# Moving the block inverses, the key and query steps and the first norm of a two-layer hybrid encoder

## The chip, the cores and the metric

The kernel runs on one core of a Trainium2 chip, as one program. The metric is the device time of one execution in microseconds (us); the time given for a kernel is the median over its runs. Besides the runs that are timed there is one profiled execution, whose trace gives start, duration and waits of every instruction. TensorE is written PE, its weight loads PEld, VectorE DVE, ScalarE ACT, GpSimd POOL and SyncE SP.

## The reference

The input is 1024 tokens of width 1024, with 16 learned tokens in front: 1040 columns. Each of two layers adds a mixer and a SwiGLU feed-forward part to the residual. The mixer has four heads of a delta rule that runs forward and backward over the sequence, and a short gated convolution beside them.

```python
h = concat([meta, x])                                   # 1040 x 1024
for l in range(2):
    y = rmsnorm(h, norm1_w[l])
    qkv, z, b, a, sc_b, sc_c, sc_h = split(y @ w_in[l])
    q, k, v = split(silu(depthwise_conv3(qkv, conv_qkv_w[l])))
    q, k = l2norm(q), l2norm(k)                         # per head of 128
    beta, g = sigmoid(b), -exp(a_log) * softplus(a + dt_bias)
    o = delta(q, k, v, g[fwd], beta[fwd]) + flip(delta(flip(q, k, v), g[bwd], beta[bwd]))
    o = o * rsqrt(mean(o * o) + eps) * dn_norm_w * silu(z)   # per head
    y_sc = sc_b * depthwise_conv3(sc_c * sc_h)
    h = h + concat([o, y_sc]) @ w_out[l]
    h = h + swiglu(rmsnorm(h, norm2_w[l]))
return rmsnorm(h, final_norm_w)[16:]

def delta(q, k, v, g, beta):       # in chunks of c rows
    G = cumsum(g);  D = exp(G_i - G_j), i >= j
    A = 1 + strictly_lower((beta k) k^T * D)
    u, w = A^-1 (beta v), A^-1 (beta k exp(G))
    attn = (q k^T * D) / sqrt(128);  qd = q exp(G) / sqrt(128)
    for each chunk:
        v_new = u - w S
        o = qd S + attn v_new
        S = S * exp(G_last) + (k exp(G_last - G))^T v_new
```

Since `q` enters `o` linearly, a factor on a query row is a factor on the output row, and the norm of the output divides it out but for `eps`.

## The kernel before

The tokens lie along the free dimension: 1040 columns, in three column chunks of 348, 346 and 346 (`FULL`; the second layer's last products use `TAIL`, without the first 16). Every large product is computed in fp32r with both operands split into a high and a low part: `dense` issues three matmuls per block of 128 input rows, 24 for one output tile of 128 and one column chunk (L154 to L156 for high by high, high by low, low by high). `wsplit` makes the weight parts, the high part on ScalarE (L127), the low part on GpSimd or, where `lov[0]` is set, on VectorE (L128).

A planner decides the order: each engine has a queue that runs in order, and the order in it is set when the kernel is built, from a priority that each instruction has when it is issued and from the planner's own idea of when its inputs are there. The code sets these priorities by hand. From the value tiles on, dense products get a low priority and serve as filling (`mmp[0]`, `low`), and evictions of them have their own (`evp[0]`). After each dense chunk `dense` pops one function from the list `jobs`, and so small work gets a place between two dense chunks.

A layer goes through these steps.

1. The norm. In the first layer the columns are scaled and split as they arrive. `add_sq` squares the eight tiles and adds them up on VectorE, GpSimd and ScalarE (L173 and near), `finish_rstd` sums over partitions with three products by a matrix of ones (L192), and the first two projections are multiplied by the result afterwards. The other norms use `finish_bc`: four column groups of a matrix of ones, then a row to memory and a broadcast back (L205).
2. The input projection, tile by tile in the order key (4 to 7), query (0 to 3), value (8 to 11), then gates `z` and the short convolution. Each tile is evicted, convolved, and passed through SiLU. `sums` (L590) adds up the squares of a key or query head; after the fourth head `normalise` takes the root, sends the row through memory to all partitions (`bc`, in a ring of two 128x1040 buffers named "c") and multiplies the four heads (L404).
3. `chunk_p` (L431), for each of nine chunks of the sequence (one of 16 columns and eight of 128): key products, decay matrix (loaded from memory, added to, four exponentials), and the product of the two for both directions. Three chunks are issued in a row.
4. `sub_start` and `substitute(d)` (L518, L520): 31 steps of two VectorE operations invert the diagonal blocks of 32 in all 32 matrices of direction d at once. For the backward direction the two 128x1024 operands (`x`) lie in the ring "c".
5. `invert(d)`: from blocks of 32 to 64 to 128. Each stage is a row of small products (L549, L555, L561 of 32x32; L573, L575 of 64x64), and evictions on ScalarE (L551, L557, L563, L577, L579) that feed the next stage. `invert(0)` is issued behind value tile 0, `substitute(1)` behind tile 1 and `invert(1)` behind tile 2, all its stages with a priority of their own ahead of the dense products.
6. `chunk_a`, for each of nine chunks: the query-key products (L474), `eg` (a broadcast load that ScalarE issues, L478) times the queries (L479), and `dt` (loaded too) times the products (L484); the results go to memory. Three chunks are issued behind each of value tiles 1 to 3.
7. The scan: `scan_step(d, c)` has chains of products with evictions between them (L762 and near). An order written by hand, below, puts three forward steps first, then mixes the directions, and ends with backward steps alone. The second layer's backward scan is one step shorter. When both directions of a chunk are there, `finalize` adds them, normalises by root mean square (four squares, root, reciprocal), turns the result and multiplies by the gate.
8. The output projection. The half that comes from the convolution channels fills TensorE during the scan; the other half (`out_part`) follows when the scan is over.
9. The second norm and the feed-forward part, as products of sums in the manner of Strassen. The change does not touch it.

```python
order = [(0, s) for s in range(3)]
for i in range(6):
    order += [(1, i), (0, 3 + i)]
order += [(1, s) for s in range(6, nb)]
```

Of the kernel before, what the change touches and what calls it, by code (L numbers as in the profile page):

```python
# [15 lines left out]
KT = 8  # L16
NMETA = 16
L = 1040
# [22 lines left out]
def trunk(ctx: ExitStack, tc: tile.TileContext, xT, w_in, w_ba, w_out, w_gu, w_dn,  # L41
# [76 lines left out]
    jobs = []  # L118
# [24 lines left out]
    def dense(ws, xs, chunks, evac, pool=None):  # L143

        for (n0, n1) in chunks:
            n = n1 - n0
            ps = (pool or pacc)()
            K = len(xs)
            here = tc.cur_priority
            if mmp[0] is not None:  # L150
                at_prio(mmp[0])
            for k in range(K):
                (wh, wl), (xh, xl) = ws[k], xs[k]
                mm(ps[:, :n], wh, xh[:, n0:n1], start=(k == 0), stop=False)  # L154
                mm(ps[:, :n], wh, xl[:, n0:n1], start=False, stop=False)  # L155
                mm(ps[:, :n], wl, xh[:, n0:n1], start=False, stop=(k == K - 1))  # L156
# [39 lines left out]
    def finish_bc(ss, n0, n1, dst):  # L196

        e = (n1 - n0) // 4
        ps = bank("a")
        for j in range(4):  # L200
            mm(ps[32 * j:32 * j + 32, 0:e], ones[:, 0:32], ss[:, n0 + e * j:n0 + e * j + e], start=True, stop=True, skip_group_check=True)
        r = c4k("r")[:, 0:e]
        act(out=r, in_=ps[:, 0:e], func=AF.Sqrt, scale=1.0 / D, bias=cols["eps"])
        nc.vector.reciprocal(out=r, in_=r)
        dma(dst[:, 0:e], r.rearrange("(a b) c -> a b c", b=32)[:, 0, :])  # L205
# [30 lines left out]
    for m in range(KT):  # L236
        add_sq(hv[m], ss, m == 0, (ptt, tt)[m % 2], m % 2 == 1, lasts[6])
# [15 lines left out]
    epsq = sb.tile([128, 1], F32, name="epsq")  # L253
    nc.vector.memset(epsq, HD * EPS)
# [5 lines left out]
    finish_rstd(ss, FULL)  # L260

    hsrc = xT
    for l in range(DEPTH):
# [129 lines left out]
        def normalise(dst, l2, r):  # L393

            scale, bias = ((float(HD), epsq), (1.0, epsc))[r > 0]
            r4 = row(Y[1] + "f")[:, 0:260]
            act(out=r4, in_=l2[:, 0:260], func=AF.Sqrt, scale=scale, bias=bias)
# [124 lines left out]
        def invert(d):  # L522
# [17 lines left out]
            def fb():  # L540
                return bank("fb"[d]).rearrange("p (q c) -> p q c", c=32)

            for qh in range(2):
                qs = slice(16 * qh, 16 * qh + 16)
                qr = range(16 * qh, 16 * qh + 16)
                ps = fb()
                for q in qr:
                    for (f, s) in pairs:
                        mm(ps[B[s], q - 16 * qh, :], P_[B[f], q, B[s]], XB[B[f], q, :], start=True, stop=True, skip_group_check=True)  # L549
                for (f, s) in pairs:  # L550
                    act(out=QS[B[s], qs, :], in_=ps[B[s]], func=AF.Copy, scale=-1.0)  # L551
                ps = fb()
                for q in qr:
                    for (f, s) in pairs:
                        mm(ps[B[f], q - 16 * qh, :], QS[B[s], q, :], P_[B[s], q, B[s]], start=True, stop=True, skip_group_check=True)  # L555
                for (f, s) in pairs:
                    act(out=P_[B[f], qs, B[s]], in_=ps[B[f]], func=AF.Copy)  # L557
                f, s = pairs[0]
                ps = fb()
                for q in qr:  # L560
                    mm(ps[B[s], q - 16 * qh, :], P_[B[s], q, B[s]], QS[B[s], q, :], start=True, stop=True)  # L561
                fo, so = 32 * (f % 2), 32 * (s % 2)
                act(out=X64[B[s], qs, fo:fo + 32], in_=ps[B[s]], func=AF.Copy)  # L563
                nc.vector.tensor_copy(X64[B[f], qs, fo:fo + 32], XB[B[f], qs, :])
                nc.vector.tensor_copy(X64[B[s], qs, so:so + 32], XB[B[s], qs, :])
                nc.vector.memset(X64[B[f], qs, so:so + 32], 0.0)

            F_, S_ = (slice(0, 64), slice(64, 128)) if d == 0 else (slice(64, 128), slice(0, 64))
            for qh in range(5):
                p1, p2 = [(bank("fb"[d]).rearrange("p (q c) -> p q c", c=64) if on else None) for on in (qh < 4, qh > 0)]  # L570
                for q in range(8):
                    if qh < 4:
                        mm(p1[S_, q, :], P_[F_, 8 * qh + q, S_], X64[F_, 8 * qh + q, :], start=True, stop=True)  # L573
                    if qh > 0:
                        mm(p2[F_, q, :], X64[S_, 8 * qh - 8 + q, :], P_[S_, 8 * qh - 8 + q, S_], start=True, stop=True)  # L575
                if qh < 4:
                    act(out=X64[S_, 8 * qh:8 * qh + 8, :], in_=p1[S_], func=AF.Copy, scale=-1.0)  # L577
                if qh > 0:
                    act(out=P_[F_, 8 * qh - 8:8 * qh, S_], in_=p2[F_], func=AF.Copy)  # L579
            at_prio(sub_end)  # L580


        l2s = {}

        def sums(which, q, sq_):
# [5 lines left out]
            if q == 3:  # L591
                normalise(*((KTt, l2s["k"], 4) if which == "k" else (QT, l2s["q"], 0)))

        seq = (4, 5, 6, 7, 0, 1, 2, 3)
        for pos, i in enumerate(seq):
# [12 lines left out]
            act(out=dst, in_=dst, func=AF.Silu)  # L608
            act(out=t, in_=dst, func=AF.Square)
            jobs.append(lambda w="qk"[i >= 4], q=hh, t=t: sums(w, q, t))  # L610
# [54 lines left out]
        for i in range(4):  # L665
            t = trow()
            inproj(8 + i, to_row(t))
# [45 lines left out]
        evp[0] = None  # L713

# [89 lines left out]
        def finalize(c, n, s0, po, pof):  # L804
# [15 lines left out]
            act(out=st[0:n], in_=st[0:n], func=AF.Sqrt, scale=1.0 / HD, bias=epsc[0:n])  # L820
# [486 lines left out]
```

## Time and profile before

| | before |
|---|---|
| median of 3 runs | 2667.32 us (2663.91 to 2669.51) |
| profiled execution | 2669.32 us, its span 2667.5 us |
| TensorE busy, weight loads | 2559.5 us (96%), 2343.7 us (88%) |
| VectorE, ScalarE, GpSimd busy | 1528.0 (57%), 988.5 (37%), 1088.5 us (41%) |
| mean granted TensorE clock | 0.981 |
| mean DMA traffic | 122 GB/s |

The page shows the span in forty slices of 66.7 us, a digit for the busy share of each in tenths; the row PEclk is the granted clock of TensorE in the same manner. Layer 0 runs from 0 to about 1380 us, layer 1 behind it. A group of the page is one line of the kernel on one engine: count, busy time, mean duration in ns, and the idle time of the engine just before its instructions, with what ended it. In a timeline the same is given for single instructions or short rows of them. Matmuls overlap, so their durations add up to more than the time that passes: of two dense products behind each other the starts are to be compared. One fp32 product of TensorE shows as two records.

### The profile page before, as it was taken

To read this page: it belongs to the slowest core of one execution; us is meant where nothing else is said; L and a number is where in the kernel's file an instruction comes from. 1 tells how busy PE (TensorE), PEld (TensorE's weight loads), DVE (VectorE), ACT (ScalarE), POOL (GpSimd) and SP (SyncE) were. 2 spreads that over 40 slices of the span, in tenths; PEclk is the share of its full clock that TensorE was granted. 3 is DMA by queue.
4 is the path that set the end of the run, shared out by engine and by line. 5 is a ranking of instruction groups with operands and counts; after the bars stand their busy time and mean duration, and the time that the engine had idled before them with its cause. 6 is when DMAs were issued, how large, how long until landed. Compare 5 with 4: busy or idle time off the path is not lost. (4 is left out here: it accounts for less than half of the span.)

```text
span 2667.5 us, 43943 instructions
## 1 busy us (share of the span) xinstructions
PE 2559.5 (96%) x17274; PEld 2343.7 (88%) x17274; DVE 1528.0 (57%) x2265; ACT 988.5 (37%) x1785; POOL 1088.5 (41%) x803
## 2 busy tenths in 40 slices
PE   8889899999999999999999998999989999999997
PEld 7889899999999999999999887898877888887886
DVE  6688333648765566522356873336497766654226
ACT  4664222425333333321246642235353333332224
POOL 3142121225766666533221321212367666663341
PEclk9999799999999999999999998999999999999999
DMA  3442685434312222532224425856232222225321
GB/s 107 143 138 83 206 252 185 144 122 138 108 60 79 85 72 76 193 111 69 73 93 142 154 76 176 280 181 207 95 126 93 68 80 77 89 88 184 93 81 64
DMA packets 181636, 326.27 MB, mean 122 GB/s; under 512 B 21696, under 2 KB 58948, under 8 KB 181428
## 3 DMA queue, kind: packets, MB, share of 16 engines
q1 hardware_dynamic: 148116, 272.77, 31.1%
q10 hardware_dynamic: 30496, 42.09, 5.2%
q0 software_dynamic: 2816, 8.59, 1.0%
q8 instruction: 136, 2.23, 0.4%
q14 instruction: 72, 0.59, 0.1%
HBM read 239.79 MB, written 83.58 MB: 121 GB/s over the span
## 5 line engine op out<-in xcount | busy, mean ns | idle before, releaser
L128 POOL TENSOR_TENSOR wlo<-raw,whi 128x512 fp32r<-128x512 f32 x244 | 294.6, 1210 | 941.2 <-ACT whi L127 857.5
L154 PE MATMUL pacc<-a,whi 128*128 128x346 f32 (+2 forms) x1031 | 347.3, 340 | 10.6 <-ACT whi L127 7.5
L127 ACT ACTIVATE whi<-raw 128x512 fp32r<-128x512 f32 (+2 forms) x264 | 151.5, 577 | 540.5 <-PE pacc L155 302.1
L156 PE MATMUL pacc<-a,wlo 128*128 128x346 f32 (+2 forms) x1031 | 347.8, 340 | 1.5 <-DVE wlo L128 0.9
L155 PE MATMUL pacc<-a,whi 128*128 128x346 f32 (+2 forms) x916 | 311.8, 341 | 1.2 <-DVE a L853 1.1
L154 PE MATMUL pacc<-b,whi 128*128 128x346 f32 (+2 forms) x882 | 303.3, 345 | 1.7 <-ACT whi L127 1.1
L156 PE MATMUL pacc<-b,wlo 128*128 128x346 f32 (+2 forms) x882 | 301.0, 344 | 0.0
L155 PE MATMUL pacc<-b,whi 128*128 128x346 f32 (+2 forms) x776 | 265.8, 343 | 1.1 <-DVE b L853 1.1
L154 PEld LDWEIGHTS pacc<-a,whi 128*128 128x128 f32 x1031 | 197.4, 192 | 22.6 <-ACT whi L127 8.7
L156 PEld LDWEIGHTS pacc<-a,wlo 128*128 128x128 f32 x1031 | 197.9, 192 | 9.9 <-DVE wlo L128 1.6
L155 PEld LDWEIGHTS pacc<-a,whi 128*128 128x128 f32 x916 | 176.1, 192 | 9.4 <-DVE a L853 1.7
L154 PEld LDWEIGHTS pacc<-b,whi 128*128 128x128 f32 x882 | 166.3, 189 | 14.9 <-issue 2.5
L156 PEld LDWEIGHTS pacc<-b,wlo 128*128 128x128 f32 x882 | 165.9, 188 | 10.4 <-issue 0.8
L996 POOL TENSOR_TENSOR wlo<-rw,whi 128x512 fp32r<-128x512 f32 x92 | 135.8, 1479 | 73.3 <-ACT whi L995 66.1
L155 PEld LDWEIGHTS pacc<-b,whi 128*128 128x128 f32 x776 | 146.6, 189 | 10.5 <-DVE b L853 1.3
L996 POOL TENSOR_TENSOR a<-rw,a 128x512 fp32r<-128x512 f32 x64 | 105.7, 1654 | 64.4 <-ACT a L995 61.7
L996 POOL TENSOR_TENSOR b<-rw,b 128x512 fp32r<-128x512 f32 x64 | 90.2, 1412 | 85.2 <-ACT b L995 54.5
L858 DVE TENSOR_TENSOR a<-pacc,a 128x346 f32<-128x346 f32 (+2 forms) x116 | 57.7, 500 | 113.6 <-PE pacc L156 112.4
L858 DVE TENSOR_TENSOR b<-pacc,b 128x512 f32<-128x512 f32 (+1 forms) x88 | 52.5, 600 | 108.4 <-PE pacc L156 107.8
L995 ACT ACTIVATE whi<-rw 128x512 fp32r<-128x512 f32 x92 | 57.8, 631 | 140.9 <-DVE rw L1069 69.9
L1070 DVE TENSOR_TENSOR rw<-raw,rw 128x512 f32<-128x512 f32 x44 | 98.0, 2227 | 1.2
L996 POOL TENSOR_TENSOR wlo<-raw,whi 128x512 fp32r<-128x512 f32 x50 | 77.5, 1552 | 34.5 <-ACT whi L995 25.9
(814 smaller groups left out, 7348.1 us busy)
## 6 DMA issues: line engine op xcount, KB each, us to landing
raw<-in_w_in SPq DMA_DIRECT2D x112, 256.0 KB, 3.0
raw<-in_w_gu SPq DMA_DIRECT2D x104, 256.0 KB, 2.7
rw<-in_w_gu SPq DMA_DIRECT2D x88, 256.0 KB, 2.6
rec<-aqd SPq DMA_DIRECT2D x62, 256.0 KB, 4.5
rec<-vkd SPq DMA_DIRECT2D x61, 256.0 KB, 2.9
raw<-in_w_dn SPq DMA_DIRECT2D x60, 256.0 KB, 2.6
raw<-in_w_out SPq DMA_DIRECT2D x48, 256.0 KB, 2.9
a<-ad SPq DMA_DIRECT2D x20, 520.0 KB, 4.6
```

What stands on the lines that cost most here:

```text
L127: act(out=hi, in_=raw[:, 0:kk, :], func=AF.Copy)
L128: (tt if lov[0] else ptt)(out=lo, in0=raw[:, 0:kk, :], in1=hi.bitcast(F32), op=ALU.subtract)
L154: mm(ps[:, :n], wh, xh[:, n0:n1], start=(k == 0), stop=False)
L155: mm(ps[:, :n], wh, xl[:, n0:n1], start=False, stop=False)
L156: mm(ps[:, :n], wl, xh[:, n0:n1], start=False, stop=(k == K - 1))
L858: tt(out=hr[m][:, n0:n1], in0=ps, in1=hr[m][:, n0:n1], op=ALU.add)
L995: act(out=hi, in_=src, func=AF.Copy)
L996: ptt(out=lo, in0=src, in1=hi.bitcast(F32), op=ALU.subtract)
L1070: tt(out=A21, in0=A11, in1=A21, op=ALU.subtract)
```

## The change

- **Inverses in pieces.** `invert(d)` no longer issues its stages. It returns seven functions: the three 32-blocked stages, each for both halves of the matrices, and the 64-blocked stages in four parts of two quarters each. They stand in the new list `jobs3`, and one is popped behind each dense chunk: those of `invert(0)` from value tile 3 on, those of `invert(1)` from the fourth of the tiles behind the values on. Their products are issued through `low`, with the priority of the dense products. `substitute(1)` is issued behind the first of these tiles.
- **Key and attention products by chunk.** `chunk_p` and `chunk_a` stand in `jobs2`, one chunk of the sequence behind each dense chunk: `chunk_p` from the fourth key tile on, `chunk_a` from value tile 2 on.
- **Queries unnormed.** The queries are not divided by their length. The sums of squares of the four heads are issued together, behind the last query tile; `query_lengths` sends the sums through memory into 36 rows of 128, turns them on TensorE, scales them and keeps them in `g`, which is free by then. `finalize` adds the length to the mean square of the output in place of `eps`.
- **First squares on TensorE.** ScalarE squares each of the eight tiles, and 32 products of 260 columns sum over partitions and tiles in one bank, in two jobs behind the second and third dense chunk; `finish_bc` goes on from there.
- **Scan order.** Four forward steps come first, and so four backward steps last (three in the second layer, before two).
- `lov[0]`, with which VectorE makes the low weight parts, stays set for the value tiles and two tiles behind them.

```diff
-            if jobs:
-                jobs.pop(0)()
+            for q in (jobs, jobs2, jobs3):
+                f = q.pop(0) if q else None
+                if f is not None:
+                    f()
...
-    def finish_bc(ss, n0, n1, dst):
+    def finish_bc(ss, n0, n1, dst, ps=None):
...
-        ps = bank("a")
-        for j in range(4):
+        sums = ps is None
+        ps = bank("a") if sums else ps
+        for j in range(4 if sums else 0):
...
-    for m in range(KT):
-        add_sq(hv[m], ss, m == 0, (ptt, tt)[m % 2], m % 2 == 1, lasts[6])
+    def first_sums(m0):
+        if m0 == 0:
+            fps.append(bank("b"))
+        for m in range(m0, m0 + 4):
+            sq = c4k("sq")
+            act(out=sq, in_=hv[m], func=AF.Square)
+            for j in range(4):
+                mm(fps[0][32 * j:32 * j + 32, 0:260], ones[:, 0:32], sq[:, 260 * j:260 * j + 260], start=(m == 0), stop=(m == KT - 1), skip_group_check=True)
+        if m0 == 4:
+            finish_bc(ss, 0, L, dram.tile([4, 260], F32, name=nm("rsd")), fps[0])
+
+    jobs.extend([None, lambda: first_sums(0), lambda: first_sums(4)])
...
-    finish_rstd(ss, FULL)
...
-            sub_end = tc.cur_priority
-            at_prio(base - 20000 + 1000 * d)
...
+            def first():
+                for qs in halves:
+                    ps = fb(32)
+                    low(lambda: [mm(ps[B[s], q - qs.start, :], P_[B[f], q, B[s]], XB[B[f], q, :], start=True, stop=True, skip_group_check=True)
+                                 for q in range(qs.start, qs.stop) for (f, s) in pairs])
                     for (f, s) in pairs:
+                        act(out=QS[B[s], qs, :], in_=ps[B[s]], func=AF.Copy, scale=-1.0)
...
+            def fourth(qh):
+                ps = fb(64)
+                low(lambda: [mm(ps[S_, q, :], P_[F_, 8 * qh + q, S_], X64[F_, 8 * qh + q, :], start=True, stop=True) for q in range(8)])
+                act(out=X64[S_, 8 * qh:8 * qh + 8, :], in_=ps[S_], func=AF.Copy, scale=-1.0)
...
+            return [first, second, third] + [lambda f=f, q=q: [f(q), f(q + 1)] for q in (0, 2) for f in (fourth, fifth)]
...
-            if q == 3:
-                normalise(*((KTt, l2s["k"], 4) if which == "k" else (QT, l2s["q"], 0)))
+            if q == 3 and which == "k":
+                normalise(KTt, l2s["k"], 4)
+            elif q == 3:
+                query_lengths(l2s["q"])
+
+        def query_lengths(l2):
+            r4 = t2k("r4").rearrange("p a b -> p (a b)")[:, 0:260]
+            nc.vector.tensor_copy(r4, l2[:, 0:260])
+            for h in range(H):
+                qdma(rnd[h].rearrange("(a c) -> a c", a=4), r4.rearrange("(a b) c -> a b c", b=32)[:, h, :])
+            rows = t2k("rows").rearrange("p a b -> p (a b)")[0:36, 0:128]
+            for h in range(H):
+                qdma(rows[9 * h:9 * h + 1, 0:16], rnd[h:h + 1, 0:16])
+                qdma(rows[9 * h + 1:9 * h + 9, :], rnd[h, 16:L].rearrange("(c p) -> c p", p=128))
+            def turn():
+                ps = pa()
+                low(lambda: nc.tensor.transpose(ps[:, 0:36], rows, ident[0:36, 0:36]))
+                ts(out=g[:, 0].rearrange("p c h -> p h c"), in0=ps[:, 0:36].rearrange("p (h c) -> p h c", h=4), scalar1=HD * EPS, scalar2=HD * EPS * EPS, op0=ALU.mult, op1=ALU.add)
+            jobs.append(turn)
...
-            if pos == 4:
+            if pos == 3:
+                jobs.append(None)
                 jobs.extend([lambda c=c: k_out(c) for c in range(9)])
-            if pos in (4, 5, 6):
-                for c in range(3 * pos - 12, 3 * pos - 9):
-                    chunk_p(c)
+                jobs2.extend([None, None] + [lambda c=c: chunk_p(c) for c in range(9)])
+
+        for hh in range(4):
+            lengths("q", hh, QT[:, hh, :], c4k("sq"))
+        qs_ = jobs[-4:]
+        del jobs[-4:]
+        jobs.extend([None, None, None, lambda: [f() for f in qs_]])
         sub_start()
         substitute(0)
...
+            if i == 2:
+                jobs2.extend([lambda c=c: chunk_a(c) for c in ca])
+            if i == 3:
+                jobs3.extend(invert(0))
             inproj(8 + i, to_row(t))
...
-            if i == 0:
-                invert(0)
-            elif i == 1:
-                substitute(1)
-                lov[0] = False
-            elif i == 2:
-                invert(1)
-            if i > 0:
-                for c in ca[3 * i - 3:3 * i]:
-                    chunk_a(c)
...
         for j, q in enumerate((4, 5, 0, 6, 7, 1, 2, 3)):
+            lov[0] = j < 2
+            if j == 3:
+                jobs3.extend(invert(1))
...
+            if j == 0:
+                substitute(1)
...
-            act(out=st[0:n], in_=st[0:n], func=AF.Sqrt, scale=1.0 / HD, bias=epsc[0:n])
+            stt(out=st[0:n], in0=st[0:n], scalar=1.0 / HD, in1=g[0:n, 0, c, :], op0=ALU.mult, op1=ALU.add)
+            act(out=st[0:n], in_=st[0:n], func=AF.Sqrt)
...
-        order = [(0, s) for s in range(3)]
-        for i in range(6):
-            order += [(1, i), (0, 3 + i)]
-        order += [(1, s) for s in range(6, nb)]
+        order = [(0, s) for s in range(4)]
+        for i in range(5):
+            order += [(1, i), (0, 4 + i)]
+        order += [(1, s) for s in range(5, nb)]
```

More of the change, by code (lines that the diff above doesn't have):

```diff
@@ L538, in invert @@
             X64 = tmp[:, 0:2, :].rearrange("p a b -> p (a b)")[:, 0:2048].rearrange("p (q c) -> p q c", q=32)
[L540 to L547, printed above, removed]
-                    for (f, s) in pairs:
[L549 to L553, printed above, removed]
+            halves = [slice(0, 16), slice(16, 32)]
@@ L554, in invert, with second @@
+            def second():
+                for qs in halves:
+                    ps = fb(32)
+                    low(lambda: [mm(ps[B[f], q - qs.start, :], QS[B[s], q, :], P_[B[s], q, B[s]], start=True, stop=True, skip_group_check=True)
+                                 for q in range(qs.start, qs.stop) for (f, s) in pairs])
                     for (f, s) in pairs:
-                        mm(ps[B[f], q - 16 * qh, :], QS[B[s], q, :], P_[B[s], q, B[s]], start=True, stop=True, skip_group_check=True)
@@ L556, in invert, with third @@
-                for (f, s) in pairs:
-                    act(out=P_[B[f], qs, B[s]], in_=ps[B[f]], func=AF.Copy)
+                        act(out=P_[B[f], qs, B[s]], in_=ps[B[f]], func=AF.Copy)
+            def third():
                 f, s = pairs[0]
-                ps = fb()
-                for q in qr:
-                    mm(ps[B[s], q - 16 * qh, :], P_[B[s], q, B[s]], QS[B[s], q, :], start=True, stop=True)
                 fo, so = 32 * (f % 2), 32 * (s % 2)
-                act(out=X64[B[s], qs, fo:fo + 32], in_=ps[B[s]], func=AF.Copy)
@@ L580, in invert @@
-            at_prio(sub_end)
+                for qs in halves:
+                    ps = fb(32)
+                    low(lambda: [mm(ps[B[s], q - qs.start, :], P_[B[s], q, B[s]], QS[B[s], q, :], start=True, stop=True) for q in range(qs.start, qs.stop)])
+                    act(out=X64[B[s], qs, fo:fo + 32], in_=ps[B[s]], func=AF.Copy)
+                    nc.vector.tensor_copy(X64[B[f], qs, fo:fo + 32], XB[B[f], qs, :])
+                    nc.vector.tensor_copy(X64[B[s], qs, so:so + 32], XB[B[s], qs, :])
+                    nc.vector.memset(X64[B[f], qs, so:so + 32], 0.0)
@@ L607, in trunk @@
             conv(t, dst, P_CV + 3 * i)
[L608 to L610 removed]
+            if i >= 4:
+                lengths("k", hh, dst, t)
             if pos == 2:
```

33 lines of the change are left out of this document (14 added, 19 removed).

## The prediction

> **What bounds the kernel now.** I read the page first, then the tables by stretch, the engine timelines of the stretches that stood out, the groups by line, and one tile. The page:
>
> ```profile
> span 2667.5 us, 43943 instructions
> PE 2559.5 (96%) x17274; PEld 2343.7 (88%) x17274; DVE 1528.0 (57%) x2265; ACT 988.5 (37%) x1785; POOL 1088.5 (41%) x803
> PEclk9999799999999999999999998999999999999999
> ```
>
> TensorE is the bound: 96% of the span, so what can be won lies in its 108 us of idle time and in the slices where the clock row falls to 7 and 8. The profiled execution took 2669.32 us, 1.8 us around its span; the median of the runs is 2667.32, 2.0 below it, so the sum below is made against 2669.32 and carried over by subtracting 2.0. The table by stretch (length, then busy time of TensorE, its weight loads, VectorE, ScalarE, GpSimd, clock, DMA share, GB/s) shows where they lie:
>
> ```profile
> 0.00:62.00 62.00, 50.47 (x274) 44.13 (x275) 44.70 (x44) 30.12 (x36) 21.20 (x14) 1.00 0.34 115
> ...
> 164.00:284.00 120.00, 113.73 (x1057) 106.88 (x1055) 98.85 (x184) 51.79 (x68) 31.05 (x26) 0.99 0.30 95
> 284.00:352.00 68.00, 57.97 (x658) 55.23 (x659) 24.25 (x36) 19.68 (x30) 8.61 (x6) 0.75 0.73 239
> 352.00:560.00 208.00, 205.90 (x1482) 199.84 (x1482) 98.49 (x231) 76.76 (x221) 47.94 (x30) 0.99 0.57 187
> ...
> 1614.00:1656.00 42.00, 32.64 (x487) 27.79 (x486) 13.32 (x17) 14.12 (x22) 4.92 (x3) 0.72 0.54 174
> ```
>
> The rows 284:352 (layer 0) and 1614:1656 (layer 1) hold the backward inverse, `invert(1)`, and stand out: 10.0 and 9.4 us idle and a granted clock of 0.75 and 0.72. The scan behind it (352:560) idles 2.1 us in 208 and needs nothing. The same table for the time at half clock:
>
> ```profile
> 293.80:321.10 27.30, 22.96 (x294) 21.38 (x293) 10.21 (x12) 13.25 (x20) 3.67 (x2) 0.50 0.59 197
> 345.00:351.80 6.80, 6.09 (x23) 6.02 (x24) 2.46 (x4) 0.00 (x0) 0.00 (x0) 0.50 1.03 332
> 1628.40:1652.30 23.90, 18.00 (x249) 16.21 (x250) 9.17 (x10) 11.34 (x17) 2.36 (x1) 0.50 0.42 138
> 300.60:307.40 6.80, 6.80 (x131) 6.74 (x130) 2.58 (x4) 3.52 (x5) 0.00 (x0) 0.50 0.65 217
> ```
>
> TensorE's timeline shows why (start, duration, what, [idle before <- who ended it]):
>
> ```profile
> 284.45 1.20 PE L549 MATMUL pb<-b,P 32*32 32x32 f32 x64 [1.65 <-DVE dt L484]
> ...
> 293.25 0.66 PE L660 MATMUL pa<-ident,b3f 128*128 128x128 f32 x4 [1.16 <-ACT b3f L661]
> 297.23 1.92 PE L549 MATMUL pb<-b,P 32*32 32x32 f32 x64 [2.73 <-ACT P L557]
> ...
> 345.70 1.65 PE L474 MATMUL pb<-b,b 128*128 128x128 f32 x6 [3.56 <-DVE dt L484]
> ...
> 1629.54 1.92 PE L549 MATMUL pb<-a,P 32*32 32x32 f32 x64 [3.19 <-ACT P L557]
> ...
> 1638.73 3.67 PE L573 MATMUL pb<-a,P 64*64 64x64 f32 x32 [1.47 <-ACT P L557]
> ```
>
> Each stage of the inverse waits for the eviction of the stage before it, with no dense product between, and its small products do not hold the clock: one stage that takes 1.20 us at 284 takes 1.92 at 297.
>
> **Inverses in seven pieces.** In the changed kernel's instruction order, TensorE has 24 dense products (one chunk of 346 columns) between any two pieces of `invert(1)`, in both layers; before, all its later stages stood in a row. What goes: layer 0, idle 10.0, and half of the busy time at half clock, (22.96 + 6.09) / 2 = 14.5, together 24.5; layer 1, 9.4 + 18.00 / 2 = 18.4. Sum 42.9 us. The work itself stays.
>
> What comes back is bounded by zero and by the same 19.4 us of waits again. I take the rate of the row 164:284, where the forward inverse already runs between dense products: 6.27 idle in 120, 5.2%, over the 110 - 43 = 67 us that the two stretches then last, 3.5 us. The clock: a piece of the first two kinds is now 64 small products without a break, two groups like the 1.20 us one at 284.45, 2.4 us. Four inverses have eight such pieces. If none trips the clock it costs 0, if each costs one step of 3.4 us at half speed (the two rows of 6.8 us are two steps each) 8 x 1.7 = 13.6. At 284.45 a single group did not trip it at once, so I take two of eight: 3.4 us.
>
> Here the Trainium skill ("TensorE: Matmul & The Clock Gate", section "What's actually happening") says that the clock halves after an idle window of about 3.4 us and comes back after a busy one. By that rule no piece could trip it, and the sum would be 3.4 us lower. The row 300.60:307.40 disagrees: busy for 6.80 of 6.80 us, in small products, at 0.50.
>
> **Key products, attention products and queries.** `chunk_p` goes from bunches of three to one behind each dense chunk at nearly the same place: nothing on the path. The larger effect comes with the queries. Before, `chunk_a` needed normalised queries, and these needed the broadcast buffers that `substitute(1)` holds; so it ran after it, on top of the inverse. Now it needs only the raw queries, and in the new order most of its multiplies stand among the 62 + 62 substitution steps on VectorE. VectorE's groups from 160 to 352 us (count | busy, mean ns | idle before, releasers):
>
> ```profile
> L520 DVE TENSOR_TENSOR b<-b,Tm 128x31 f32<-128x31 f32 (+15 forms) x31 | 15.6, 502 | 0.7
> L520 DVE TENSOR_TENSOR x<-x,Tm 128x31 f32<-128x31 f32 (+15 forms) x31 | 14.8, 476 | 0.9
> ...
> L518 DVE TENSOR_TENSOR Tm<-b 128x31 f32<-128x31 f32 (+15 forms) x31 | 12.5, 404 | 0.7
> L518 DVE TENSOR_TENSOR Tm<-x,x 128x31 f32<-128x31 f32 (+15 forms) x31 | 11.5, 371 | 0.9
> L479 DVE TENSOR_TENSOR eg<-b,eg 128x512 f32<-128x512 f32 x13 | 9.3, 719 | 19.3 <-DMA eg<-ged 14.6 <-DMA aqd<-eg 2.6 <-issue 2.0
> L484 DVE TENSOR_TENSOR dt<-pb,dt 128x512 f32<-128x512 f32 x13 | 8.8, 688 | 19.3 <-PE pb L474 10.0 <-DMA dt<-dtd 5.9 <-issue 2.8
> L404 DVE TENSOR_TENSOR b<-b,bc 128x1040 f32<-128x1040 f32 x4 | 5.4, 1360 | 4.0 <-DMA bc<-rnd 4.0
> ...
> L128 DVE TENSOR_TENSOR wlo<-raw,whi 128x512 fp32r<-128x512 f32 x1 | 0.7, 692 | 0.2 <-ACT whi L127 0.2
> ```
>
> Is VectorE then the bound? In 164:284 it is busy 98.85 us. Added: 32 large multiplies of `chunk_a` at 0.70, 22.4 (some 3 us of them were in the stretch), eight weight splits moved over from GpSimd at 0.69, 5.5; removed, the four query multiplies, 5.4. That makes about 119 us. TensorE's own time for the stretch up to the backward inverse grows from 120 to about 134: the order has 49 more dense products there (7.8 us at 0.16 each) and some 24 chunk products and 24 transposes (about 6). VectorE stays some 15 us ahead, so I cost the move at nothing; the cover is those 15 us. The two new query transposes are 0.3 us (four transposes take 0.66 at 293.25). The length in the output norm is one 128x4 operation in each of 17 steps, behind the scan's dense products. GpSimd's queue gets twelve small transfers for four 128x1040 ones; the turn that needs them stands some 200 products later, so nothing waits.
>
> **First squares on TensorE.** The rows of the old way, and what a group of four 260-column sums costs:
>
> ```profile
> 28.07 0.43 PE L155 MATMUL pacc<-a3f,whi 128*128 128x348 f32 x1 [2.28 <-DVE a3f L173]
> ...
> 40.45 0.85 PE L192 MATMUL pa<-rstd,ones 128*128 128x348 f32 x2 [0.20 <-DVE rstd L184]
> 41.14 1.33 PE L192 MATMUL pb<-rstd,ones 128*128 128x346 f32 x4
> ```
>
> ```profile
> 1394.26 0.33 PE L154 MATMUL pacc<-b,whi 128*128 128x346 f32 x1
> 1394.42 0.32 PE L155 MATMUL pacc<-b,whi 128*128 128x346 f32 x1
> 1394.67 0.65 PE L590 MATMUL pf<-a,sel 128*32 128x260 f32 x8
> 1395.24 0.43 PE L156 MATMUL pacc<-b,wlo 128*128 128x346 f32 x1
> 1395.51 0.32 PE L154 MATMUL pacc<-b,whi 128*128 128x346 f32 x1
> ```
>
> From L155 at 1394.42 to the second dense product behind it, at 1395.51, it is 1.09 us; without the sums it would be two steps of 0.16 (1394.26 to 1394.42). A group adds 0.77, eight 6.2; the three old sums, 2.0, go, and the 2.28 wait goes because VectorE no longer squares between the splits. Of the 11.5 us idle in 0:62, the sums can fill some. Against it, the norm now goes through memory. As at the next layer's norm,
>
> ```profile
> 1368.88 0.52 SPq L205 DMA_DIRECT2D rsd<-r  x1
> ```
>
> ```profile
> 1374.38 1.26 DVE L605 TENSOR_TENSOR a<-a,rstd 128x1040 f32<-128x1040 f32 x1 [1.21 <-DMA rstd<-rsd]
> ```
>
> 5.5 us pass before its first use, and on ScalarE's queue a weight cast for the third tile stands behind the first convolution that needs it: I reckon TensorE waits about 2.5 us. All of it on the path gives +6.7 (6.2 - 2.0 + 2.5), all of it in idle time -5; I take -1.
>
> **Sum.** 2669.3 - 42.9 + 3.5 + 3.4 + 0.3 - 1 = 2632.6, and 2.0 less for the median: 2630.6 us, a gain of 36.7. Its own range, 2620 to 2648: below, no waits and no half clock (-6.9) and the start at its best (-4); above, half of the waits and of the trips return, (19.4 + 13.6) / 2 - 6.9 = 9.6, and the start at its worst, 7.7.
>
> **Rivals.**
> A, slower: the multiplies of `chunk_a` take their waits along. The two groups above wait 38.6 us in layer 0 for their loads and products; VectorE's queue runs in order, so the substitution behind them waits too, and then every piece of the inverse. It decides from 15 us of such waits in a layer, and the kernel is slower from 15 + 36.7 / 2 = 33. At the full 38.6 it is 2 x (38.6 - 15) = 47 us: 2678. ScalarE issues the loads, and the tile `eg` shows who stood behind them:
>
> ```profile
>   ACT whi L127: 17.6, 3
>   ACT P L557: 7.3, 1
> ```
>
> Against it: those loads ran at a DMA share of 0.73, in a stretch of 68 us; now they spread over one with 0.30. The skill's same page ("Architectural detail: the array is 16× 32×32, not 1× 128×128") calls ScalarE's and VectorE's queues strict in order, which is the rule that speaks against this change; the rows agree.
> B, half the gain: each of the eight long pieces costs two steps at half clock, 16 x 1.7 = 27 instead of 3.4: 2654. For it, the half clock held from 293.8 to 321.1 once begun; against it, dense products now follow each piece.
> C, no change: the scan gives it back. The new order ends with four steps of the backward scan alone, where there were three.
>
> ```profile
> 519.38 1.05 PE L762 MATMUL pb<-vv,P 128*128 128x128 f32 x8
> ...
> 536.04 0.82 PE L762 MATMUL pb<-vv,P 16*16 16x128 f32 x6
> ```
>
> Such a step takes 16.7 us. If the dense products left over don't cover the extra one in either layer, 33 us return: 2664. Against it: at the scan's end twelve of 24 chunks of the output projection are still left in layer 0; in layer 1 none are, so half of it is likelier than all.
>
> **Chances.** Forecast 0.62; A 0.10; B 0.17; C 0.11. About 0.2%, 5 us, is what a measurement can tell from no change. Faster: the forecast, B and half of C, 0.84; same 0.06; slower, A, 0.10. The range 2612 to 2662 holds the forecast, B and half of C.
>
> **What would show it.** Right: no stretch at half clock longer than 7 us in either mixer; the row for the backward inverse at clock 0.95 or more; two fewer waits of L484 on TensorE; the first scan product some 30 us earlier, since it stands behind the inverse. Wrong: VectorE idle inside the substitution with DMA as releaser (A); many single steps at half clock right behind the 32-column pieces (B); waits of the scan's products at the start of the second output projection (C).

## The result and the profile after

| | before | after |
|---|---|---|
| median (lowest to highest, runs) | 2668.07 us (2663.91 to 2669.51, 4) | 2631.88 us (2631.29 to 2632.31, 4) |
| ratio, 95% interval | | 0.9867 [0.985, 0.9884] |
| profiled execution, span | 2669.32, 2667.5 us | 2631.29, 2629.5 us |
| TensorE busy, idle in the span | 2559.5, 108.0 us | 2547.8, 81.7 us |

The change makes the kernel 36.2 us faster. (The kernel before was run once more, so its median is 2668.07 and not the 2667.32 that the forecast was made from.) The page of the changed kernel:

```profile
span 2629.5 us, 44056 instructions
PE 2547.8 (97%) x17334; PEld 2331.2 (89%) x17334; DVE 1486.3 (57%) x2281; ACT 978.9 (37%) x1779; POOL 1057.5 (40%) x792
PEclk9999999999999999999999999999999999999999
```

Of the 38 us of span, 26.3 are idle time of TensorE. The rest is busy time, 11.7 us less although 31 products came in: the mean granted clock rose from 0.981 to 0.99. The slices with 7 and 8 are gone. VectorE has 16 instructions more and is 41.7 us less busy. The table by stretch, with the columns of before:

```profile
0.00:62.00 62.00, 52.23 (x315) 41.59 (x316) 27.85 (x33) 34.10 (x41) 13.33 (x13) 0.97 0.38 128
...
164.00:284.00 120.00, 117.24 (x1109) 113.39 (x1108) 107.67 (x223) 46.96 (x65) 19.36 (x21) 0.99 0.64 211
284.00:352.00 68.00, 68.00 (x781) 64.72 (x780) 11.85 (x24) 24.13 (x42) 19.14 (x13) 1.00 0.43 134
352.00:560.00 208.00, 203.13 (x1443) 197.99 (x1442) 99.05 (x235) 70.40 (x209) 42.86 (x28) 0.98 0.46 149
...
1614.00:1656.00 42.00, 42.00 (x553) 36.66 (x552) 3.81 (x6) 14.60 (x23) 8.03 (x8) 1.00 0.38 116
```

The two rows of the backward inverse are without idle time and at full clock, where before TensorE was idle for 10.0 and 9.4 us at a clock of 0.75 and 0.72. What came in elsewhere is small: the scan (352:560) idles 4.9 us instead of 2.1, and two places of layer 1 have waits. TensorE's timeline there (1428.44 and 1546.59), at the weights of the third tile (44.90) and at the first forward piece of layer 0 (220.90):

```profile
44.90 0.43 PE L154 MATMUL pacc<-a,whi 128*128 128x348 f32 x1 [2.46 <-ACT whi L127]
...
220.90 2.21 PE L558 MATMUL pf<-b,P 32*32 32x32 f32 x128 [0.70 <-DVE b L542]
...
1428.44 0.28 PE L425 MATMUL pa<-ident,a 128*16 128x128 f32 x1 [3.35 <-DVE a L417]
...
1546.59 3.63 PE L558 MATMUL pf<-a,P 32*32 32x32 f32 x128 [5.25 <-DVE a L542]
```

L542 is the turn of the inverted 32-blocks on VectorE, the last step ahead of the pieces.

### The profile page after: what moved, and what is told of

Its sections match the earlier page's. It is cut to its first block, busy times and chain, and to the rows that moved or that the text cites. A ratio compares the mean times of both kernels' runs of the same rounds, so it can differ in the third digit from the quotient of the medians.

```text
span 2629.5 us, 44056 instructions
## 1 busy us (share of the span) xinstructions
PE 2547.8 (97%) x17334; PEld 2331.2 (89%) x17334; DVE 1486.3 (57%) x2281; ACT 978.9 (37%) x1779; POOL 1057.5 (40%) x792
## 5 line engine op out<-in xcount | busy, mean ns | idle before, releaser
L128 POOL TENSOR_TENSOR wlo<-raw,whi 128x512 fp32r<-128x512 f32 x228 | 271.3, 1192 | 981.1 <-ACT whi L127 818.1
L156 PEld LDWEIGHTS pacc<-b,wlo 128*128 128x128 f32 x882 | 166.9, 189 | 10.2 <-issue 0.8
L1110 DVE TENSOR_TENSOR rw<-rw,rw 128x512 f32<-128x512 f32 x44 | 65.7, 1493 | 51.2 <-POOL wlo L1041 34.5
```

The source lines that it names most:

```text
L128: (tt if lov[0] else ptt)(out=lo, in0=raw[:, 0:kk, :], in1=hi.bitcast(F32), op=ALU.subtract)
L1110: tt(out=s1t, in0=A21, in1=A22, op=ALU.add)
```

## The experiments

Chips differ by several us (the kernel before has medians from 2667.6 to 2673.8), so each run is read by its ratio to the kernel before on the same chip. The changed kernel itself has 0.9867 above and was run twice more beside others, with 0.9831 and 0.9857. That spread, 0.36% or 10 us, is as large as some of the differences below.

### Is it the dense products between the pieces?

The first run issues the seven pieces of the backward inverse as one job:

```diff
-                jobs3.extend(invert(1))
+                back = invert(1)
+                jobs3.append(lambda: [f() for f in back])
```

> The changed kernel, with the seven pieces of the backward inverse issued as one job: in a row on TensorE, no dense chunk between them, in both layers. Everything else stays. Theory (the dense chunks between the pieces are the gain): the waits and the half clock come back, 24.5 us in layer 0 and 18.4 us in layer 1, so about 2632 + 43 = 2675 us, at least 2660, with two stretches of over 15 us at half clock. Rival (the gain is the earlier attention products, the raw queries and the lighter GpSimd, and the row of pieces is harmless once these are out of its way): within 10 us of 2632, and no stretch at half clock over 7 us there.

Measured: 2625.32 us (2620.36 to 2628.1), ratio 0.9838 [0.9823, 0.9853]: not slower than the changed kernel. But the run does not decide between the two, since it was no row: TensorE's order has 17 to 21 dense products between the pieces, put there by the planner. How the code hands out the pieces does not matter there. A later run forces the row, beside the changed kernel.

> The changed kernel itself, on the chip of the next three runs. 2632 us; a difference of 2 us or less from that is the spread of the chips.

Measured: 2628.56 us, ratio 0.9831 [0.9813, 0.9849], 3.4 us below what was expected.

To force the row, the first product of every later dense chunk is made to wait for the last product of the pieces:

```diff
-                mm(ps[:, :n], wh, xh[:, n0:n1], start=(k == 0), stop=False)
+                ins = mm(ps[:, :n], wh, xh[:, n0:n1], start=(k == 0), stop=False)
+                if k == 0 and gate[0] is not None:
+                    after(ins, gate[0])
...
+                    gate[0] = lastmm[0]
```

> The first run in a row was none: issued as one job, the pieces of the backward inverse still had 17 to 21 dense products between them in TensorE's order, put there by the planner. Here every dense chunk issued behind the pieces depends on their last product, so that the order has no dense product between them, in both layers. Theory one (dense products between the pieces are the gain, whoever puts them there): six evictions of 2 to 3 us uncovered in each layer and their small products at half clock, so 15 to 25 us a layer: 2662 to 2680 us. Theory two (the stretch was slow for want of dense products, because their weights stood behind loads on ScalarE's queue, and the row itself is cheap): under 10 us a layer, 2635 to 2650 us.

Measured: 2649.69 us, ratio 0.991 [0.9893, 0.9926]: 21.1 us slower than the changed kernel beside it. As a total that lies just inside theory two's range, though it is 10.6 us a layer, over that theory's 10. Of theory one's two terms the half clock came, and the uncovered evictions did not. TensorE's timeline of the row in layer 0, and the table of the stretches ahead of, in and behind the half clock:

```profile
291.51 2.09 PE L561 MATMUL pb<-b,P 32*32 32x32 f32 x120
293.87 2.41 PE L569 MATMUL pb<-P,b 32*32 32x32 f32 x128 [0.27 <-ACT b L564]
...
297.34 2.71 PE L579 MATMUL pb<-b,P 32*32 32x32 f32 x47 [0.26 <-issue]
299.98 3.35 PE L590 MATMUL pb<-b,P 64*64 64x64 f32 x29
```

```profile
293.00:297.00 4.00, 3.64 (x183) 3.27 (x177) 0.00 (x0) 3.81 (x8) 0.00 (x0) 1.00 0.34 137
297.00:317.48 20.48, 20.22 (x194) 19.96 (x192) 0.00 (x0) 6.42 (x11) 0.00 (x0) 0.50 0.18 57
317.48:321.50 4.02, 4.02 (x30) 3.58 (x30) 0.52 (x1) 0.51 (x2) 0.00 (x0) 1.00 0.44 147
1624.80:1645.28 20.48, 20.48 (x231) 19.53 (x226) 0.00 (x0) 7.75 (x14) 0.00 (x0) 0.50 0.10 29
```

The evictions are hidden behind the other half of each stage (idle 0.27 and 0.26), but the clock falls, and stays at 0.50 for 20.48 us in each layer: 2 x 20.48 / 2 = 20.5 of the 21.1 us. So dense products between the small ones are worth about 21 us here, nearly all of it clock. The new form evicts one half of the matrices while it multiplies the other; a row of the old form, which goes through its stages one half behind the other, was not run without the attention products beside it, so this run alone does not say where the 19.4 us of idle time before came from.

### Where did the waits come from?

> The changed kernel, with the nine chunks of attention products not behind value tile 2 but issued together with the backward inverse, one behind each dense chunk, so that their loads and multiplies share the stretch of the inverse as they did before. Theory one (dense products between the pieces are the gain): they are still there in TensorE's order (20 and more), so within 8 us of 2632. Theory two (the loads on ScalarE's queue starve the dense products): waits of dense products for the weight casts in that stretch, half clock there, 20 us or more slower, 2652 or more. Under both the forward substitution on VectorE loses 18 multiplies and their waits, so the first piece of the forward inverse in layer 1 no longer waits its 5.25 us.

Measured: 2626.27 us, ratio 0.9821 [0.9802, 0.984]. Its table by stretch:

```profile
284.00:352.00 68.00, 66.61 (x676) 62.73 (x670) 22.93 (x36) 15.50 (x25) 12.78 (x9) 1.00 0.74 242
...
1614.00:1656.00 42.00, 39.04 (x356) 35.85 (x356) 13.08 (x21) 8.20 (x13) 9.17 (x6) 0.96 0.75 235
```

The DMA share in the first row is that of before (0.73), yet TensorE is busy for 66.6 of 68 us at full clock. So the loads at this place, one chunk of attention products behind each dense chunk, do not starve the stretch, and theory two is out. The loads are not free, though. In layer 1 TensorE idles 3.0 us, for an eviction of the inverse (L588) that stands behind loads on ScalarE; ScalarE's timeline (ACTq is the issue of a load):

```profile
1650.54 0.33 ACTq L491 DMA_DIRECT2D eg<-ged  x1
1650.91 0.59 ACT L588 ACTIVATE a<-pb 64x512 f32<-64x512 f32 x1 [7.13 <-DMA aqd<-dt]
```

The forward wait in layer 1 went, as both theories had it; the total is that of the changed kernel beside it (0.9821 against 0.9831) within the spread.

The pieces alone, in the kernel before (`invert(0)` and `invert(1)` both in the new form; one line of several):

```diff
...
-                invert(1)
+                jobs3.extend(invert(1))
...
```

> The kernel before, with one part of the change alone: both inverses in pieces, one behind each dense chunk (the forward one behind value tile 0, the last two parts in one; the backward one behind value tile 2, as before). Key and attention products, queries, first squares and scan order as before. The order then has 14 to 45 dense products between the pieces of the backward inverse in layer 0, but for the 64-blocked ones, some of which stand together; in layer 1 8 to 43. Theory one (the pieces are the gain): 30 to 40 us faster than before, 2628 to 2638. Theory two (the attention products behind normalised queries had to be taken out of the stretch): 0 to 15 us faster, 2652 to 2667, with waits for weight casts and half clock left in the stretch.

Measured: 2684.63 us, ratio 1.0042 [1.0028, 1.0057]: slower. Both theories miss; the first is out. TensorE's timeline shows the first pieces of both layers:

```profile
302.35 1.92 PE L547 MATMUL pb<-b,P 32*32 32x32 f32 x64 [7.17 <-DVE dt L485]
...
1639.44 1.92 PE L547 MATMUL pb<-a,P 32*32 32x32 f32 x64 [10.29 <-DVE dt L485]
```

The backward pieces take banks of the ring "b", and so do the query-key products of `chunk_a`, whose banks come free with the multiply by `dt`. These multiplies come in a burst at this very place, since the queries are normed late. Pieces in a strict order behind them wait longer.

The third way round, the queries alone: the old inverses, the old bursts, only no norm of the queries. `query_lengths` and the length in `finalize` are those of the change.

```diff
-            if q == 3:
-                normalise(*((KTt, l2s["k"], 4) if which == "k" else (QT, l2s["q"], 0)))
+            if q == 3 and which == "k":
+                normalise(KTt, l2s["k"], 4)
+            elif q == 3:
+                query_lengths(l2s["q"])
...
```

> The kernel before, with one part of the change alone: the queries are not normed, their length goes into the output norm. The inverses keep their old form and places, with no pieces, and the attention products their bursts of three. In the order that the planner makes of it, 16 to 24 dense products stand between all stages of the backward inverse in both layers, where the kernel before has almost none. Theory three (the normed queries were the cause: the attention products had to wait for the buffers that the backward substitution holds, and so met the backward inverse): most of the gain comes from this part alone, 30 us or more, 2643 or less, no half clock over 7 us in the two stretches. Theory one (the pieces are the gain): none of it, within 8 us of the kernel before.

Measured: 2648.31 us (2641.04 to 2652.59), ratio 0.9903 [0.9884, 0.9922]; the changed kernel beside it:

> The changed kernel itself, beside the three others on their chip: 2628 to 2633 us.

Measured: 2633.1 us, 0.9857 [0.984, 0.9874]. So the queries alone bring 24.7 of 40.0 us: theory one is out, and it is less than theory three said. The first large multiply of the attention products by `eg` starts at 199.7 us, where the kernel before has it at 275.5. The table by stretch of this run has both inverses healed, without a piece:

```profile
164.00:284.00 120.00, 109.76 (x1162) 102.93 (x1162) 97.10 (x192) 53.72 (x71) 29.86 (x28) 0.97 0.40 130
284.00:352.00 68.00, 68.00 (x666) 65.98 (x664) 18.51 (x29) 18.94 (x30) 16.31 (x12) 1.00 0.55 181
...
1614.00:1656.00 42.00, 42.00 (x388) 35.44 (x382) 6.46 (x10) 12.96 (x20) 11.00 (x8) 1.00 0.34 112
```

In TensorE's order dense products now stand between the old stages (16 to 24, but for the third, which follows the second), where the kernel before has at most 2 between most of them. Why the planner orders it so is not shown; it decides by its own idea of when inputs are there.

With this the trace of the kernel before can be read again. Of the 19.4 us of idle time in its two stretches, 4.5 end with a multiply by `dt`, which frees a bank, and 12.3 with an eviction of the inverse itself. The two longest of these, 2.73 and 3.19 us, are for evictions that stood behind loads of the attention products on ScalarE and so came late. ScalarE's timeline of the kernel before:

```profile
295.61 0.33 ACTq L478 DMA_DIRECT2D eg<-ged  x1
295.99 0.59 ACT L557 ACTIVATE P<-pb 32x512 f32<-32x512 f32 x1 [2.79 <-DMA aqd<-dt]
...
1627.91 0.35 ACTq L483 DMA_DIRECT2D dt<-dtd  x1
1628.30 1.19 ACT L557 ACTIVATE P<-pb 32x512 f32<-32x512 f32 x2 [7.34 <-DVE eg L479]
```

About half of the 15.3 us that are missing against the changed kernel is idle time ahead of the inverses: 164:284 and 1380:1614 together idle 8.2 us more than in the changed kernel beside it. TensorE's timeline of the queries alone, and VectorE's just before:

```profile
217.41 0.66 PE L154 MATMUL pacc<-a,whi 128*128 128x348 f32 x1 [6.49 <-DVE b L279]
```

```profile
214.05 0.69 DVE L479 TENSOR_TENSOR eg<-b,eg 128x512 f32<-128x512 f32 x1 [3.90 <-DMA eg<-ged]
...
215.33 0.69 DVE L484 TENSOR_TENSOR dt<-pb,dt 128x512 f32<-128x512 f32 x1 [0.36 <-DMA dt<-dtd]
...
216.85 0.51 DVE L279 TENSOR_TENSOR b<-pacc,rstd 128x348 f32<-128x348 f32 x1
```

VectorE waits 3.90 us for a load of a burst; the eviction of a dense chunk stands behind it, and TensorE waits for its bank. In layer 1 the same costs 6.08 us at 1530.63. This is rival A's mechanism. The changed kernel, with one chunk of attention products behind each dense chunk, idles 4.3 us in 164:284 where this run idles 10.2, and 9.6 instead of 11.9 in 1380:1614. That the spreading by chunk does this was not tried by itself.

> The kernel before with two parts: queries not normed, and the inverses in pieces as in the run of the pieces alone. Theory three: the pieces add little to the queries alone, within 6 us of that run. Theory one in a weaker form (pieces need the raw queries, and then bring about half): 12 us or more faster than the queries alone.

Measured: 2652.73 us, ratio 0.9927 [0.9911, 0.9943]. Pieces on top of the raw queries bring nothing (4.4 us slower, the intervals overlap), as theory three had it. The changed kernel with the old form of the inverses was not run.

### The other parts

The low weight parts, given back to GpSimd:

```diff
-            lov[0] = j < 2
...
+            if i == 1:
+                lov[0] = False
```

> The changed kernel, but the low weight parts of value tiles 2 and 3 and of the two tiles behind them are made by GpSimd again, as before (16 subtractions of 128x512). Theory (a VectorE operation that meets such a GpSimd operation is stretched, by up to 1.1 us; in the kernel before 49 such meetings cost 40 us, after the change 35 cost 26 us): VectorE's total busy time does not fall by the 11 us of the moved operations but stays or rises, and the wait of the first forward piece in layer 1 (5.25 us) stays or grows: 2632 to 2637. Rival (the moved operations are a load on VectorE, as the prediction counted them, 5.5 us in a layer): the forward substitution ends 4 to 5 us earlier, the 5.25 us wait goes, and with it some half clock: 2622 to 2626.

Measured: 2648.84 us, ratio 0.9929 [0.9913, 0.9946], against 0.9831 to 0.9867 for the changed kernel: 0.6 to 1.0%, 16 to 26 us. The rival is out. VectorE's busy time rises as the theory said, 1495.6 instead of 1486.3 us, but the loss is far above its 0 to 5 us, and the wait of the first forward piece in layer 1 is 1.36 us and did not grow. VectorE's groups from 160 to 352 us, first of this run, then of the changed kernel:

```profile
L531 DVE TENSOR_TENSOR Tm<-b 128x31 f32<-128x31 f32 (+15 forms) x31 | 14.5, 468 | 0.5
...
L533 DVE TENSOR_TENSOR b<-b,Tm 128x31 f32<-128x31 f32 (+15 forms) x31 | 12.2, 392 | 0.6
```

```profile
L533 DVE TENSOR_TENSOR b<-b,Tm 128x31 f32<-128x31 f32 (+15 forms) x31 | 10.4, 337 | 0.5
L531 DVE TENSOR_TENSOR Tm<-b 128x31 f32<-128x31 f32 (+15 forms) x31 | 10.4, 336 | 0.5
```

Without the subtractions of two tiles VectorE is not ahead: the forward substitution takes 26.7 instead of 20.8 us busy. TensorE idles 11.7 of these 192 us instead of 2.8, 6.3 of them behind multiplies by `dt`. How the rest of the size comes about stays open.

The old scan order, three forward steps first:

```diff
-        order = [(0, s) for s in range(4)]
...
+        lead = 3
+        order = [(0, s) for s in range(lead)]
...
```

> The changed kernel with the old scan order, three forward steps first and three (two in layer 1) backward steps last. Theory from the two traces (layer 0 of the changed kernel waits 1.67 and 2.33 us near 507 us with 6.8 us at half clock, before it had 3.4 us at half clock there; layer 1 before waited 2.45 and 1.12 us near 1860 us, after it nothing): layer 0 gains 5 to 6 us, layer 1 loses 3 to 4, together 2629 to 2631. Rival (an added backward step alone costs its full length of 16.7 us in a layer): 2632 - 16 = 2616 or less. Rival (the order does nothing): 2632.

Measured: 2640.25 us, ratio 0.9896 [0.9882, 0.991]: 0.3 to 0.65%, 8 to 17 us slower than the changed kernel. All expectations miss, down to the sign. The tables by stretch, of this run and of the changed kernel, show the end of layer 0's scan:

```profile
513.60:537.49 23.89, 20.35 (x73) 14.73 (x72) 8.94 (x17) 5.68 (x23) 6.46 (x2) 0.50 0.32 124
```

```profile
507.70:514.50 6.80, 5.55 (x20) 5.55 (x21) 5.18 (x10) 1.81 (x9) 0.00 (x0) 0.50 0.92 347
```

With the rest of the change, three steps leave 23.9 us at half clock there, four 6.8. Half of the difference, some 8.5 us, is what the clock costs there at most. Why three steps leave more is not settled.

The first norm as it was:

```diff
-    jobs.extend([None, lambda: first_sums(0), lambda: first_sums(4)])
+    for m in range(KT):
+        add_sq(hv[m], ss, m == 0, (ptt, tt)[m % 2], m % 2 == 1, lasts[6])
...
+    finish_rstd(ss, FULL)
```

> The changed kernel with the first norm as it was before: squares on VectorE, GpSimd and ScalarE, three sums on TensorE, no row through memory. Theory from the two traces (dense product 216 starts at 64.2 us before and 66.2 us after the change): 2 us faster than the changed kernel, 2630. The prediction's value: 1 us slower, 2633. Rival (the new sums fill idle time that VectorE's squares would open again beside the earlier key products): 5 us slower or more, 2637.

Measured: 2638.35 us, ratio 0.9887 [0.9873, 0.9902]: slower by 0.2 to 0.6%, 5 to 15 us, if the chips agree to that. The first of the gate products, which stand behind the third tile, show the start; TensorE's timeline of this run, and of the changed kernel:

```profile
49.58 2.55 PE L343 MATMUL pacc<-a,P 128*32 128x348 f32 x15 [0.85 <-DVE b L295]
```

```profile
53.28 1.58 PE L341 MATMUL pacc<-a,P 128*32 128x348 f32 x9
59.29 1.11 PE L341 MATMUL pacc<-a,P 128*32 128x348 f32 x6
```

So the new way is late by then, and is repaid later; by what stays open, as the planner's order differs behind that point.

The parts do not add up. Left out one at a time, these three cost at least 5, 8 and 16 us, together more than the 15.3 us that the changed kernel has over the queries alone; what one is worth depends on the others.

Last, a try for more:

> An attempt at a faster version: the changed kernel with the attention products issued together with the backward inverse, as in the run before, and in layer 1 the turns of the keys one dense chunk later, so that they do not wait for the normalised keys (3.35 us near 1428 us, with 3.4 us at half clock). If both effects stay, 2 + 5 us faster than the changed kernel on the same chip. If the scan gives back what is won ahead of it, as it did with the attention products, 2 us.

Measured: 2634.12 us, ratio 0.9858 [0.9838, 0.9877], the changed kernel beside it 0.9857. No better version. In 164:284 TensorE idles 0.5 us, where the changed kernel beside it has 4.3, but nothing of that shows in the time; where it is given back was not followed.

## Why the prediction was right

The time, 2630.6 against 2631.88 us, and the gain, 36.7 against 36.2, are right, and so is the sum's large term: the 42.9 us of the two stretches went, whole. How close it came is in part luck, since some terms were wrong in opposite ways. By its own steps:

- **What goes.** Right in its two sizes and in what was missing, dense products between the stages; wrong in what takes them away. Half clock, 23.5 us in the sum: the forced row brings 20.5 back. Idle, 19.4 us: 12.3 of it do end with an eviction of the inverse, as the prediction read it, but the longest of these came late behind loads of the attention products, and 4.5 end with a multiply by `dt`. The attention products were in the backward inverse's place, in its banks and ahead of its evictions, because the queries were normed late. The prediction saw this order ("so it ran after it, on top of the inverse") and gave it no term; raw queries alone bring 24.7 us.
- **Inverses in seven pieces.** This step failed: the pieces as such bring nothing, neither in the kernel before (0.4% slower) nor with raw queries. With the queries out of the way the planner puts dense products between the old stages too.
- **Waits that come back, 3.5 us.** The term was for the stretches of the backward inverse, and there it is 0. The forward inverse, which had no such term, waits 0.70 us in layer 0 and 5.25 in layer 1.
- **Half clock, 3.4 us for two of eight long pieces.** Two windows, 3.4 us long at 224.4 and 10.2 at 1545.4, both at or just behind the first forward piece, which waits for VectorE; they cost up to half of it, 6.8. None of the other pieces shows half clock in this trace.
- **VectorE 15 us ahead.** At the backward inverse it was ahead, by less: its last turn in layer 0 ends at 281.39 us, and the first piece starts at 290.03 without a wait. At the forward inverse, which the sum did not ask about, it was not: TensorE waits 0.70 and 5.25 us there. On the other side, the moved weight splits were a load of 5.5 us a layer by the sum, and relieved VectorE instead.
- **First squares, -1 us.** The wait of 2.5 us on ScalarE's queue came as reckoned (2.46 at 44.90). The kernel with the old squares is 5 to 15 us slower, but its order differs further on as well, so whether the term itself is -1 can't be told.
- **Scan.** The sum put the fourth step at nothing and rival C at a loss of up to 33 us. With the rest of the change it helps, by 8 to 17 us.
- The errors offset each other, which the 1.3 us between forecast and result hides. Of what would show it, the two rows at clock 1.00 came. So did two fewer waits of TensorE for the multiply by `dt` (two instead of four) and an earlier scan (its first product starts at 336.4 us instead of 375.6). The stretches at half clock came as stated but for the 10.2 us in layer 1. The rows at clock 1.00 came with the raw queries alone too, so that sign could not tell the two apart.

## What to carry to other kernels

A stretch where many small things wait is not explained by the thing that sits in it: ask which of them came there late, and why; here a ring of two buffers made the queries late (in layer 0 of the kernel before, GpSimd sits idle for 9.7 us before the first broadcast of their lengths, until the copies that free a backward operand are done). Before cutting work into pieces by hand, see whether the planner fills the gaps once something is ready. An experiment with one part alone shows what a right number hides.

## What the runs showed of the hardware

In the forced row the clock fell under small products and stayed at 0.50 while TensorE was busy for 20.22 of 20.48 us in layer 0 and for all of 20.48 in layer 1 (above). The Trainium skill ("TensorE: Matmul & The Clock Gate", section "What's actually happening") has the clock halve after an idle window of about 3.4 us; in the forced row no idle time is over 0.3 us in layer 0 or over 0.5 in layer 1, and the measurement decides. What the clock follows instead no run here shows.

An operation of the substitution on VectorE, with two operands in SBUF, that started while GpSimd ran a subtraction of two fp32 tiles of 128x512 ended only 0.2 us behind it. The timelines of GpSimd and VectorE in the kernel before:

```profile
172.56 1.30 POOL L128 TENSOR_TENSOR wlo<-raw,whi 128x512 fp32r<-128x512 f32 x1 [18.52 <-ACT whi L127]
```

```profile
172.60 1.43 DVE L518 TENSOR_TENSOR Tm<-b 128x156 f32<-128x156 f32 x1
174.06 0.32 DVE L520 TENSOR_TENSOR b<-b,Tm 128x156 f32<-128x156 f32 x1
```

The substitution's other operation of the same shape takes 0.32 us right behind it. The Trainium skill ("SBUF — State Buffer", section "Who interferes with whom") says that a VectorE instruction with two inputs in SBUF contends with a GpSimd instruction that reads SBUF, and that the one issued later is blocked; the trace agrees. The prediction had counted the moved subtractions as load alone: they take 0.69 us on VectorE, and 1.30 on GpSimd, where an operation of VectorE can stand behind them.
